# A transformer block on one core: the first transfer joined with part of x^T, and the norm of attention B one step behind its products

## The chip, the core and the metric

The kernel runs on one core of a Trainium2 chip. The metric is device time in microseconds (us) of one execution, as the median over several runs. The changed kernel is compared with the kernel before on the same chip.

## What is computed

One layer of an encoder block on a sequence of 512 rows of 1024 (S = 512, D = 1024), all in float32. Cut to what matters:

```python
proj = u @ w_in                          # [q_a|k_a|v_a | q_b|k_b|v_b | g], 5120 columns
o_a  = chunked_relbias_attention(q_a, k_a, v_a, rel_bias)     # 8 heads of 64
# attention B: 4 heads, two softmax maps each, values 128 wide
s1, s2 = q1 @ k1.T * scale, q2 @ k2.T * scale   # q, k with partial rotary, masked by chunk
w    = softmax(s1) - lam * softmax(s2)
o_b  = rms_norm(w @ v_b, subln_g) * (1.0 - lam_init)          # per head and row
gates = sigmoid(g + b_gate)
mix  = (g_a * (o_a @ w_branch_a) + g_b * (o_b @ w_branch_b)) @ w_out
x    = LN1(alpha * x + mix)
x    = LN2(alpha * x + relu(x @ w_ff1)**2 @ w_ff2)
```

## The kernel before, in words

**Products in three parts.** Every float32 operand is split into a high and a low part (`split`, lines 83 to 87: ACT casts, line 84; DVE subtracts, line 85), and a product is the sum of three matmuls: high by high, high by low, low by high (`tmm`, lines 184 to 186, with the weights held; `smm`, lines 189 to 191, with the activations held). The weights are one stream `w` of chunks of 128 x 1024 in the order of their use. `prefetch` loads and splits them ahead (tiles `raw`, `wh`, `wl`, three buffers each); `chunk` hands out the next. In a group by `smm` (`s_group`) four row tiles run over blocks of x^T of 128 rows (tiles X): block 0 for all four row tiles, then block 1, and so on, so the first 12 matmuls use block 0.

**The start.** `warm_up(7)` (line 252) sends seven matmuls of zeros. `first_loads` issues, on ACT's queue, the first 128 columns of block 0 of x^T (line 113), and on SP's queue the first half of chunk 0, the other 384 columns of that block, the second half of chunk 0, block 1, and so on. `split_x` splits block 0 in two pieces (line 100), since the first products need only 128 columns of it.

**The main line of work** is `proj` (values of A, then four pairs of query and key of A, queries, keys and values of B, eight pairs of gates, and branch A), a generator that stops after every 12 matmuls or so. `advance(n)` lets it do n such steps. The attention's steps are put between: 36 steps of `attn_a`, then `attn_b`, with PACE = 1.8 steps of the main line to each (line 678). The engines work in order. A scheduler puts each engine's instructions in order at build time, starting from the order of the code; it may move one ahead of or behind its neighbours on the same engine.

**Attention B** (`attn_b`, lines 505 to 583) has 16 units (head h, row tile t). Unit i is begun in step i: two score products (277, 278), for each map the sum with the mask and its maximum (`softexp`, line 285, DVE), Exp (287, ACT) and reciprocal (289, DVE); then the second map times lam/sum: a scalar product on DVE (563), a scaling on POOL (564), and the combination on DVE (565). LAG = 3 steps later `prob_transpose` transposes the result on PE (296) and splits it (303 ACT, 304 DVE). In the unit t = 2 of a head `prep_b` transposes the queries and keys of the next (500) and `stack` splits them (261 ACT, 262 DVE).

Two further stages follow once the last row tile of a head is through. Stage 1, one step later, is `pv` (520 to 522): the products with the values, and from them on ACT the square twice (525, and 526 as `sq_h`) and `og` (528), and on DVE the low part of the square, `sq_l` (529). Stage 3, two steps behind that, is `normalise`: two matmuls with `ones_r` (536), the first over `sq_h`, the second over `sq_l`, give the mean square in every row; then Sqrt on ACT (537, with a load of its function table before and one after, for Exp), the reciprocal on DVE (538, 3.35 us), the product with `og` (541) and its split. The loop:

```python
for stage in (3, 1):
    k = i - LAG - stage
    if 0 <= k < len(units) and k % NT == NT - 1:
        h = units[k][0]
        if stage == 1:
            held[h] = pv(h)
        else:
            normalise(*held.pop(h))
```

Of the kernel before, what the change touches and what calls it, by code (L numbers as in the profile page):

```python
# [9 lines left out]
F32 = mybir.dt.float32  # L10
# [6 lines left out]
P = 128  # L17
# [23 lines left out]
def block_kernel(ctx, tc, w, x_t, x, pos, relb, bgate, lq1, lk1, lq2, lk2, subg,  # L41
# [56 lines left out]
    def split_x(k):  # L98
        h, l, raw = xt(FR), xt(FR), x_raw.pop(k)
        for lo, hi in ((0, P), (P, S)) if k == 0 else ((0, S),):  # L100
            split(raw[:, lo:hi], h[:, lo:hi], l[:, lo:hi])
        xh.append(h)
        xl.append(l)
# [7 lines left out]
    def first_loads():  # L111

        load_x(0, ((0, P),), A)
        for i in range(2):
            raws[i] = wp.tile([P, 1024], F32, tag="raw", bufs=3, name=name("raw"))
            for j in range(2):
                sl = slice(512 * j, 512 * (j + 1))
                nc.sync.dma_start(out=raws[i][:, sl], in_=w[i][:, sl])
                load_x(2 * i + j, ((P, S),) if i + j == 0 else ((0, S),))
        dma_at[0] = 2  # L120

    def prefetch(n_dma, n_split):
# [5 lines left out]
        while split_at[0] < min(NCH, n_split):  # L128
# [7 lines left out]
            else:  # L136
                h = wp.tile([P, 1024], FR, tag="wh", bufs=3, name=name("wh"))
                l = wp.tile([P, 1024], FR, tag="wl", bufs=3, name=name("wl"))
                if i < 2:
                    for j in range(2):  # L140
                        sl = slice(512 * j, 512 * (j + 1))
                        split(raws[i][:, sl], h[:, sl], l[:, sl])
                        split_x(2 * i + j)
                else:
                    split(raws[i], h, l, G if i in on_pool else V)
# [42 lines left out]
    def smm(ps, ah, al, w_h, w_l, first, last):  # L188
        T.matmul(ps, ah, w_h, start=first, stop=False)  # L189
        T.matmul(ps, ah, w_l, start=False, stop=False)  # L190
        T.matmul(ps, al, w_h, start=False, stop=last)  # L191
# [313 lines left out]
    def attn_b():  # L505
# [44 lines left out]
        for i in range(len(units) + LAG + 4):  # L550
# [24 lines left out]
            for stage in (3, 1):  # L575
# [100 lines left out]
    for _ in range(16 + LAG + 4):  # L676
        next(steps_b, None)
        due += PACE
        advance(int(due))
        due -= int(due)  # L680
# [259 lines left out]
def _layout(x, positions, w_in, b_gate, rel_bias, lambda_q1, lambda_k1, lambda_q2, lambda_k2,  # L940
            subln_g, w_branch_a, w_branch_b, w_out, ln1_g, ln1_b, w_ff1, w_ff2, ln2_g, ln2_b):
    a = {k: np.asarray(v) for k, v in locals().items()}
    idx = np.clip(384 + np.arange(P)[:, None] - np.arange(S)[None, :], -128, 128) + 128
    return {
        "w": _weight_stream(a["w_in"][0], a["w_branch_a"][0], a["w_branch_b"][0], a["w_out"][0],
                            a["w_ff1"][0], a["w_ff2"][0]),
        "x_t": a["x"][0].T,
# [29 lines left out]
```

## Time and profile before

| what | value |
|---|---|
| median of 3 runs | 736.63 us (736.24 to 737.06) |
| the profiled execution, its own time | 734.53 us |
| its span on the core | 732.7 us |
| mean granted clock of TensorE | 0.996 of full speed |
| busy: PE / DVE / ACT / POOL | 98% / 59% / 40% / 12% |

The page of the profile gives the busy time of each engine (PE is TensorE's matmuls, PEld its weight loads, DVE VectorE, ACT ScalarE, POOL GpSimd, SP the engine that issues most transfers). The waits list says which instruction of an engine stood idle for which instruction of another. The timeline lists instructions by their start; the names in it are the program's tiles without their numbers, and L529 is line 529 of the kernel. A matmul of 512 columns shows some 0.39 us in the timeline although the next starts 0.23 us later, since neighbours overlap.

### The profile page before, as it was taken

To read this page: it belongs to the slowest core of one execution; us is meant where nothing else is said; L and a number is where in the kernel's file an instruction comes from. 1 tells how busy PE (TensorE), PEld (TensorE's weight loads), DVE (VectorE), ACT (ScalarE), POOL (GpSimd) and SP (SyncE) were. 2 spreads that over 40 slices of the span, in tenths; PEclk is the share of its full clock that TensorE was granted. 3 is DMA by queue.
4 is the path that set the end of the run, shared out by engine and by line. 5 is a ranking of instruction groups with operands and counts; after the bars stand their busy time and mean duration, and the time that the engine had idled before them with its cause. 6 is when DMAs were issued, how large, how long until landed. Compare 5 with 4: busy or idle time off the path is not lost.

```text
span 732.7 us, 9157 instructions
## 1 busy us (share of the span) xinstructions
PE 721.3 (98%) x3415; PEld 603.0 (82%) x3415; DVE 432.0 (59%) x788; ACT 295.7 (40%) x512; POOL 89.3 (12%) x119
## 2 busy tenths in 40 slices
PE   9999999999999999999999999999999999999995
PEld 7888888888887888888898888888888888888885
DVE  6676655547667767655877885423225655622545
ACT  6465654546567755334453322212112322312200
POOL 0022323231433120042000000000000000000001
PEclk9999999999999999999999999999999999999998
DMA  8663222222332313364213223233232223232302
GB/s 291 212 181 100 87 87 65 80 87 84 111 94 76 98 58 115 125 249 159 73 59 111 79 98 115 87 97 104 87 109 92 87 86 115 90 111 87 116 29 87
DMA packets 27085, 78.35 MB, mean 107 GB/s; under 512 B 4384, under 2 KB 5152, under 8 KB 27040
## 3 DMA queue, kind: packets, MB, share of 16 engines
q1 hardware_dynamic: 26176, 76.64, 32.0%
q10 hardware_dynamic: 864, 1.11, 0.4%
q8 instruction: 27, 0.44, 0.2%
q14 instruction: 18, 0.15, 0.1%
HBM read 71.45 MB, written 2.10 MB: 100 GB/s over the span
## 4 chain that ended last, share of the span: by engine, by line
PE 95%; DVE 2%; ACT 1%; issue 1%; DMA 0%; POOL 0%; DVEq 0%; POOLq 0%; ACTq 0%
PE mm L184 11%; PE mm L186 11%; PE mm L185 11%; PE mm L189 9%; PE mm L190 9%; PE mm L191 9%; PE st L190 4%; PE st L191 4%; PE st L189 4%; PE st L185 3%; PE st L184 3%; PE st L186 3%; PE o L190 2%; PE o L191 1%; PE o L189 1%; PE st L278 1%
## 5 line engine op out<-in xcount | busy, mean ns | idle before, releaser
L85 DVE TENSOR_TENSOR wl<-raw,wh 128x1024 fp32r<-128x1024 f32 (+1 forms) x116 | 140.2, 1209 | 121.7 <-ACT wh L84 121.4
L84 ACT CAST wh<-raw 128x1024 fp32r<-128x1024 f32 (+1 forms) x116 | 120.1, 1035 | 193.7 <-PE st L191 67.1
L189 PE MATMUL mm<-wh,X 128*128 128x512 f32 (+1 forms) x192 | 76.7, 400 | 1.1 <-ACT wh L84 0.8
L184 PE MATMUL mm<-X,wh 128*128 128x512 f32 x192 | 76.9, 401 | 0.0
L185 PE MATMUL mm<-X,wh 128*128 128x512 f32 x192 | 75.0, 390 | 0.0
L186 PE MATMUL mm<-X,wl 128*128 128x512 f32 x192 | 74.9, 390 | 0.0
L190 PE MATMUL mm<-wl,X 128*128 128x512 f32 (+1 forms) x192 | 74.5, 388 | 0.0
L191 PE MATMUL mm<-wh,X 128*128 128x512 f32 (+1 forms) x192 | 74.4, 388 | 0.0
L186 PE MATMUL mm<-x1t_h,wl 128*128 128x512 f32 x128 | 49.8, 389 | 0.0
L185 PE MATMUL mm<-x1t_l,wh 128*128 128x512 f32 x128 | 49.8, 389 | 0.0
L184 PE MATMUL mm<-x1t_h,wh 128*128 128x512 f32 x128 | 49.8, 389 | 0.0
L287 ACT ACTIVATE e<-e,s 128x128 f32<-128x128 f32 (+3 forms) x64 | 36.1, 564 | 33.6 <-DVE s L285 32.1
L771 POOL TENSOR_SCALAR s<-s 128x1 f32<-128x1 f32 x1 | 0.4, 409 | 388.2 <-DVE s L755 388.2
L379 POOL TENSOR_SCALAR e<-e,s 128x128 f32<-128x128 f32 (+3 forms) x32 | 34.7, 1086 | 84.5 <-DVE s L289 84.5
L189 PEld LDWEIGHTS mm<-wh,X 128*128 128x128 f32 x192 | 36.1, 188 | 8.7 <-ACT wh L84 1.3
L186 PEld LDWEIGHTS mm<-X,wl 128*128 128x128 f32 x192 | 36.1, 188 | 7.8
L191 PEld LDWEIGHTS mm<-wh,X 128*128 128x128 f32 x192 | 36.1, 188 | 7.6
L184 PEld LDWEIGHTS mm<-X,wh 128*128 128x128 f32 x192 | 36.1, 188 | 6.9
L185 PEld LDWEIGHTS mm<-X,wh 128*128 128x128 f32 x192 | 36.1, 188 | 6.6
L190 PEld LDWEIGHTS mm<-wl,X 128*128 128x128 f32 x192 | 36.2, 188 | 6.5
L84 ACT CAST V<-lt 128x512 fp32r<-128x512 f32 x24 | 14.9, 620 | 62.5 <-DVE lt L849 62.5
L186 PE MATMUL st<-x1t_h,wl 128*128 128x512 f32 (+1 forms) x104 | 38.8, 373 | 0.0
(254 smaller groups left out, 1545.8 us busy)
## 6 DMA issues: line engine op xcount, KB each, us to landing
raw<-in_w_dram SPq DMA_DIRECT2D x118, 512.0 KB, 3.3
q<-q SPq DMA_DIRECT2D x32, 128.0 KB, 2.3
G<-in_relb_dram SPq DMA_DIRECT2D x8, 256.0 KB, 4.6
x<-in_x_dram SPq DMA_DIRECT2D x4, 512.0 KB, 6.5
e<-in_x_t_dram SPq DMA_DIRECT2D x7, 256.0 KB, 6.3
raw<-in_w_dram SPq DMA_DIRECT2D x4, 256.0 KB, 4.6
out_dram<-x SPq DMA_DIRECT2D x3, 256.0 KB, 2.1
out_dram<-x ACTq DMA_DIRECT2D x3, 256.0 KB, 2.1
```

The source lines that it names most:

```text
L84: A.copy(out=h, in_=src)
L85: i = (eng or V).tensor_tensor(out=l, in0=src, in1=h.bitcast(F32), op=ALU.subtract)
L184: T.matmul(ps, lw_h, rh, start=first, stop=False)
L185: T.matmul(ps, lw_h, rl, start=False, stop=False)
L186: T.matmul(ps, lw_l, rh, start=False, stop=last)
L189: T.matmul(ps, ah, w_h, start=first, stop=False)
L190: T.matmul(ps, ah, w_l, start=False, stop=False)
L191: T.matmul(ps, al, w_h, start=False, stop=last)
L278: T.matmul(ps[:, :n], q2[:, sl], k1[:, :n], start=False, stop=True)
L287: A.activation(e[:, :n], e[:, :n], AF.Exp, bias=nm, scale=-1.0, accum_out=sums)
L379: G.tensor_scalar(ex[:, :n], ex[:, :n], r, None, op0=ALU.mult)
L771: G.tensor_scalar(nmr, mv[:, 0:1], -1.0, None, op0=ALU.mult)
```

## The change

Three edits.

1. **The first transfer.** A new input `w_x` holds, side by side, the first half of chunk 0 (512 columns) and the first 128 columns of block 0 of x^T. One transfer of 640 columns on SP's queue brings both into the tile `raw` of chunk 0; the transfer on ACT's queue is gone. The second half of chunk 0 goes into a tile of its own (`half`). `first_split` casts the 128 columns of x and half of the weights on DVE, the other half of the weights on ACT; the subtractions follow on DVE.
2. **The order in `smm`**: high by high, low by high, high by low.
3. **The norm of attention B** moves from stage 3 to stage 2, one step behind `pv`, and the loop is one step shorter.

The diff, cut to its core:

```diff
     def split_x(k):
         h, l, raw = xt(FR), xt(FR), x_raw.pop(k)
-        for lo, hi in ((0, P), (P, S)) if k == 0 else ((0, S),):
-            split(raw[:, lo:hi], h[:, lo:hi], l[:, lo:hi])
+        split(raw, h, l)
...
     def first_loads():
-        load_x(0, ((0, P),), A)
         for i in range(2):
             raws[i] = wp.tile([P, 1024], F32, tag="raw", bufs=3, name=name("raw"))
             for j in range(2):
                 sl = slice(512 * j, 512 * (j + 1))
-                nc.sync.dma_start(out=raws[i][:, sl], in_=w[i][:, sl])
-                load_x(2 * i + j, ((P, S),) if i + j == 0 else ((0, S),))
+                if i + j == 0:
+                    nc.sync.dma_start(out=raws[0][:, 0:640], in_=w_x)
+                    half.append(e_tile())
+                    load_x(0, ((P, S),))
+                elif i == 0:
+                    nc.sync.dma_start(out=half[0], in_=w[0][:, sl])
+                    load_x(1)
+                else:
+                    nc.sync.dma_start(out=raws[i][:, sl], in_=w[i][:, sl])
+                    load_x(2 * i + j)
...
+    def first_split(h, l):
+        raw, x0h, x0l = raws[0], xt(FR), xt(FR)
+        V.tensor_copy(out=x0h[:, 0:P], in_=raw[:, 512:640])
+        A.copy(out=h[:, 0:256], in_=raw[:, 0:256])
+        V.tensor_copy(out=h[:, 256:512], in_=raw[:, 256:512])
+        V.tensor_tensor(out=x0l[:, 0:P], in0=raw[:, 512:640], in1=x0h[:, 0:P].bitcast(F32),
+                        op=ALU.subtract)
+        V.tensor_tensor(out=l[:, 0:512], in0=raw[:, 0:512], in1=h[:, 0:512].bitcast(F32),
+                        op=ALU.subtract)
+        split(x_raw.pop(0)[:, P:S], x0h[:, P:S], x0l[:, P:S])
...
+        split(half.pop(), h[:, 512:1024], l[:, 512:1024])
+        split_x(1)
...
     def smm(ps, ah, al, w_h, w_l, first, last):
         T.matmul(ps, ah, w_h, start=first, stop=False)
-        T.matmul(ps, ah, w_l, start=False, stop=False)
-        T.matmul(ps, al, w_h, start=False, stop=last)
+        T.matmul(ps, al, w_h, start=False, stop=False)
+        T.matmul(ps, ah, w_l, start=False, stop=last)
...
-        for i in range(len(units) + LAG + 4):
+        for i in range(len(units) + LAG + 3):
...
-            for stage in (3, 1):
+            for stage in (2, 1):
...
-    for _ in range(16 + LAG + 4):
+    for _ in range(16 + LAG + 3):
...
+        "w_x": np.concatenate([w[0][:, 0:512], x_t[0:P, 0:P]], 1),
```

The lines of the changed kernel stand 27 further down from `smm` on (line 529 before is 556 after, 536 is 563, 565 is 592). What the scheduler makes of edit 3 shows in the orders of the engines.

PE in head 0 of attention B before, behind the scores of a unit of head 1 (st) and the transposes of the same step (L296); the rows behind them are gate products:

```order
L277 MATMUL st_2431<-q_2282,q_2271 128x128
L278 MATMUL st_2431<-q_2282,q_2288 128x128
L296 MATMUL mm_2445<-ident,e_2198 128x128 x2
L184 MATMUL mm_2450<-X_136,wh_2172 128x512
L185 MATMUL mm_2450<-X_137,wh_2172 128x512
L186 MATMUL mm_2450<-X_136,wl_2173 128x512
```

The same place with the change:

```order
L304 MATMUL st_2432<-q_2283,q_2272 128x128
L305 MATMUL st_2432<-q_2283,q_2289 128x128
L323 MATMUL mm_2446<-ident,e_2199 128x128 x2
L563 MATMUL mm_2451<-V_2370,ones_r 128x512
L563 MATMUL mm_2451<-V_2371,ones_r 128x512
L211 MATMUL mm_2462<-X_134,wh_2173 128x512
L212 MATMUL mm_2462<-X_135,wh_2173 128x512
L213 MATMUL mm_2462<-X_134,wl_2174 128x512
```

The two ones-products (L563; V are the two parts of the square) now stand straight behind the transposes, ahead of the gate products, which follow unmoved.

Where the pair stood before on PE, one step further down, behind three transposes:

```order
L277 MATMUL st_2493<-q_2282,q_2271 128x256
L278 MATMUL st_2493<-q_2282,q_2288 128x256
L296 MATMUL mm_2507<-ident,e_2242 128x128 x3
L536 MATMUL mm_2513<-V_2369,ones_r 128x512
L536 MATMUL mm_2513<-V_2370,ones_r 128x512
L184 MATMUL mm_2536<-X_136,wh_2384 128x512
L185 MATMUL mm_2536<-X_137,wh_2384 128x512
```

With the change these transposes (L323) are followed by the gate products at once; 24 gate products lie between the two places.

DVE in head 2 before, around the last unit's softmax (L285, L289), the scalar of its second map (L563), the low part of the square (L529) and the combination (L565, which reads what POOL scaled in line 564):

```order
L289 RECIPROCAL s_2927<-s_2924 128x1
L285 ISA e_2932,s_2933<-st_2929,maskb 128x512
L285 ISA s_2933 128x1
L289 RECIPROCAL s_2937<-s_2934 128x1
L563 TENSOR_SCALAR s_2939<-s_2937,lam 128x1
L529 TENSOR_TENSOR V_2964<-e_2962,V_2963 128x512
L565 SCALAR_TENSOR_TENSOR e_2922<-e_2922,s_2927,e_2932 128x512
L85 TENSOR_TENSOR wl_2998<-raw_2989,wh_2997 128x1024
```

The same place with the change (L316 is 289 before, L312 is 285, L331 is 304, L590 is 563, L592 is 565, L556 is 529):

```order
L316 RECIPROCAL s_2928<-s_2925 128x1
L312 ISA e_2933,s_2934<-st_2930,maskb 128x512
L312 ISA s_2934 128x1
L331 TENSOR_TENSOR pl_2945<-mm_2946,ph_2944 128x128
L316 RECIPROCAL s_2938<-s_2935 128x1
L590 TENSOR_SCALAR s_2940<-s_2938,lam 128x1
L592 SCALAR_TENSOR_TENSOR e_2923<-e_2923,s_2928,e_2933 128x512
L556 TENSOR_TENSOR V_2965<-e_2963,V_2964 128x512
L85 TENSOR_TENSOR wl_3010<-raw_3001,wh_3009 128x1024
```

The low part of the square has moved from ahead of the combination to behind it. In head 0 it stands behind the combination in both kernels, in head 1 the change puts it ahead of the reciprocal and the scalar.

DVE at the start before (X_136 and X_137 are the high and low parts of block 0 of x^T, X_145 the low part of block 1):

```order
L249 MEMSET e_101 128x128
L85 TENSOR_TENSOR X_137<-e_110,X_136 128x128
L85 TENSOR_TENSOR wl_133<-raw_112,wh_132 128x512
L85 TENSOR_TENSOR X_137<-e_110,X_136 128x384
L85 TENSOR_TENSOR wl_133<-raw_112,wh_132 128x512
L85 TENSOR_TENSOR X_145<-e_116,X_144 128x512
```

And with the change (X_134 and X_135 are block 0 now, X_146 the low part of block 1):

```order
L276 MEMSET e_101 128x128
L134 CAST X_134<-raw_110 128x128
L136 CAST wh_132<-raw_110 128x256
L137 TENSOR_TENSOR X_135<-raw_110,X_134 128x128
L139 TENSOR_TENSOR wl_133<-raw_110,wh_132 128x512
L85 TENSOR_TENSOR X_135<-e_113,X_134 128x384
L85 TENSOR_TENSOR wl_133<-e_112,wh_132 128x512
L85 TENSOR_TENSOR X_146<-e_116,X_145 128x512
```

Two casts and one subtraction now stand ahead of the first low part of the weights (wl); the low part of block 1 is still last.

## Rows read from the trace of the kernel before

**Rows 1.** The page, part 1: busy us of each engine, share, instructions.
```profile
PE 721.3 (98%) x3415; PEld 603.0 (82%) x3415; DVE 432.0 (59%) x788; ACT 295.7 (40%) x512; POOL 89.3 (12%) x119
```
**Rows 2.** Waits of PE: waiter <- releaser: us in all, times, longest.
```profile
PE mm L296 <- DVE pl L304: 1.4, 1, 1.4
PE st L252 <- DVE e L249: 1.0, 1, 1.0
PE mm L189 <- ACT wh L84: 0.8, 1, 0.8
```
**Rows 3.** DMA issues of the first 3 us: KB each, median us to landing.
```profile
raw<-in_w_dram SPq DMA_DIRECT2D x1, 256.0 KB, 3.2
e<-in_x_t_dram ACTq DMA_DIRECT2D x1, 64.0 KB, 3.4
...
e<-in_x_t_dram SPq DMA_DIRECT2D x1, 256.0 KB, 4.5
```
**Rows 4.** Timeline of the start: start us, us, engine, instruction, idle time before it.
```profile
4.11 0.30 ACT L84 CAST X<-e 128x128 fp32r<-128x128 f32 x1 [1.67 <-DMA e<-in_x_t_dram]
4.32 0.61 ACT L84 CAST wh<-raw 128x512 fp32r<-128x512 f32 x1
...
4.98 0.92 PE L189 MATMUL mm<-wh,X 128*128 128x512 f32 x2 [0.77 <-ACT wh L84]
...
7.33 0.69 DVE L85 TENSOR_TENSOR X<-e,X 128x512 fp32r<-128x512 f32 x1
...
8.32 0.39 PE L190 MATMUL mm<-wl,X 128*128 128x512 f32 x1
```
**Rows 5.** Groups of DVE by form: busy us, mean ns, idle before.
```profile
L440 DVE COPY cos_t<-cos_t 128x32 f32<-128x32 f32 x1 | 0.2, 180 | 0.6 <-ACT cos_t L436 0.6
L442 DVE COPY cos_t<-cos_t 128x64 f32<-128x64 f32 x1 | 0.2, 196 | 0.0
```
**Rows 6.** Timeline: head 0's reciprocal, and PE's wait behind it.
```profile
227.99 3.35 DVE L538 RECIPROCAL e<-e 128x512 f32<-128x512 f32 x1 [1.08 <-ACT e L537]
...
236.76 0.33 PE L296 MATMUL mm<-ident,e 128*128 128x128 f32 x1 [1.37 <-DVE pl L304]
```
**Rows 7.** Timeline: POOL and DVE in head 0, up to `sq_l`.
```profile
216.37 1.56 POOL L564 TENSOR_SCALAR e<-e,s 128x512 f32<-128x512 f32 x1 [7.44 <-DVE s L563]
217.97 0.94 DVE L565 SCALAR_TENSOR_TENSOR e<-e,s,e 128x512 f32<-128x512 f32 x1 [1.79 <-POOL e L564]
218.83 0.80 DVE L529 TENSOR_TENSOR V<-e,V 128x512 fp32r<-128x512 f32 x1
```
**Rows 8.** Timeline of PE in head 0: the new place of the pair, and the old.
```profile
217.24 0.48 PE L184 MATMUL mm<-X,wh 128*128 128x512 f32 x1
...
223.52 0.72 PE L536 MATMUL mm<-V,ones_r 128*128 128x512 f32 x2
224.08 0.40 PE L184 MATMUL mm<-X,wh 128*128 128x512 f32 x1
```
**Rows 9.** Timeline of PE, DVE and POOL in head 2.
```profile
269.62 0.48 PE L184 MATMUL mm<-X,wh 128*128 128x512 f32 x1
...
271.24 0.69 DVE L529 TENSOR_TENSOR V<-e,V 128x512 fp32r<-128x512 f32 x1
271.36 2.00 POOL L564 TENSOR_SCALAR e<-e,s 128x512 f32<-128x512 f32 x1 [4.82 <-ACT V L526]
...
273.39 0.75 DVE L565 SCALAR_TENSOR_TENSOR e<-e,s,e 128x512 f32<-128x512 f32 x1 [1.47 <-POOL e L564]
```
**Rows 10.** Timeline: first scores of head 2's last unit, and their softmax.
```profile
264.03 0.39 PE L278 MATMUL st<-q,q 128*128 128x512 f32 x1
...
267.12 0.68 DVE L285 CUSTOM_DVE_ANT_0 e<-st,maskb 128x512 f32<-128x512 f32 x1
```
**Rows 11.** Busy us by stretch (PE, PEld, DVE, ACT, POOL), PE's granted clock, DMA share, GB/s.
```profile
237.00:239.00 2.00, 2.00 (x14) 1.86 (x14) 1.91 (x5) 1.98 (x5) 0.25 (x1) 1.00 0.91 199
```
**Rows 12.** Timeline of PE: the warm-up.
```profile
1.04 3.17 PE L252 MATMUL st<-e 128*128 128x512 f32 x7 [1.04 <-DVE e L249]
```

More of the change, by code (lines that the diff above doesn't have):

```diff
@@ L40, in block_kernel @@
 @with_exitstack
-def block_kernel(ctx, tc, w, x_t, x, pos, relb, bgate, lq1, lk1, lq2, lk2, subg,
+def block_kernel(ctx, tc, w, w_x, x_t, x, pos, relb, bgate, lq1, lk1, lq2, lk2, subg,
                  ln1_g, ln1_b, ln1_gt, ln1_bt, ln2_g, ln2_b, out):
@@ L117, in first_loads @@
                 sl = slice(512 * j, 512 * (j + 1))
-                nc.sync.dma_start(out=raws[i][:, sl], in_=w[i][:, sl])
-                load_x(2 * i + j, ((P, S),) if i + j == 0 else ((0, S),))
-        dma_at[0] = 2
+                if i + j == 0:
[8 more added lines that the diff above has]
+                    load_x(2 * i + j)
+        dma_at[0] = 2
+    half = []
+    def first_split(h, l):
[8 more added lines that the diff above has]
+        split(x_raw.pop(0)[:, P:S], x0h[:, P:S], x0l[:, P:S])
+        xh.append(x0h)
+        xl.append(x0l)
+        split(half.pop(), h[:, 512:1024], l[:, 512:1024])
+        split_x(1)
     def prefetch(n_dma, n_split):
@@ L138, in prefetch @@
                 l = wp.tile([P, 1024], FR, tag="wl", bufs=3, name=name("wl"))
-                if i < 2:
+                if i == 0:
+                    first_split(h, l)
+                elif i == 1:
                     for j in range(2):
@@ L943, in _layout @@
     idx = np.clip(384 + np.arange(P)[:, None] - np.arange(S)[None, :], -128, 128) + 128
+    w = _weight_stream(a["w_in"][0], a["w_branch_a"][0], a["w_branch_b"][0], a["w_out"][0],
+                       a["w_ff1"][0], a["w_ff2"][0])
+    x_t = a["x"][0].T
     return {
-        "w": _weight_stream(a["w_in"][0], a["w_branch_a"][0], a["w_branch_b"][0], a["w_out"][0],
-                            a["w_ff1"][0], a["w_ff2"][0]),
-        "x_t": a["x"][0].T,
+        "w": w,
+        "w_x": np.concatenate([w[0][:, 0:512], x_t[0:P, 0:P]], 1),
+        "x_t": x_t,
         "x": a["x"][0],
```

## The prediction

> **What bounds the kernel now.** I read the page's busy times first, then the waits of PE, then the timelines of PE, DVE, ACT and POOL at the few places where PE waits. PE is busy for 721.3 of 732.7 us [rows 1]: nearly everything is TensorE work, and only what makes PE start later or stand still can move the end. PE has three waits of over half a us [rows 2]: 1.0 us before the warm-up matmuls, 0.8 us before the first real one, and 1.4 us once in attention B. (The rest of its idle time is the tail behind the last matmul, which the change leaves alone.) So at most 0.8 us at the start and 1.4 us in attention B are to be had, and the question is which new waits come.
>
> The profiled execution took 734.53 us, 732.7 of it span; the median of the runs shown is 736.63, 2.10 above. I make the sum against 734.53 and add the 2.10 at the end. About 0.2% (1.5 us) is what a measurement of this kernel tells from no change.
>
> **Part 1, the start.** Before, 128 columns of `x^T` are issued on ACT's queue and land 3.4 us later, and the first half chunk on SP's lands 3.2 us after its issue [rows 3]. ACT casts x at 4.11 (0.30 us), then the half chunk at 4.32 (0.61 us), and PE's first product starts at 4.98, 0.05 behind the cast's end [rows 4]. The change puts both in one transfer of the same bytes. I let it land at 4.1, as x does. ACT then casts 256 columns, which takes between 0.30 (for 128) and 0.61 (for 512), say 0.4, while DVE casts 128 and then 256. A one-source DVE copy takes 180 ns for 32 columns and 196 for 64 [rows 5], 0.5 ns a column: 0.23 and 0.29 us by that. PE's first product could start at 4.1 + 0.23 + 0.29 + 0.05 = about 4.7, 0.3 us earlier.
>
> It does not keep all of that. In the new order the second product of each three takes the low part of x, so the second product of the second block of x (the 14th in all) needs that low part; before, only the 15th did. The block comes by an unchanged transfer, 4.5 us on its way [rows 3], and its low part is made at 7.33 and ready at 8.02 [rows 4]. PE can therefore run its 14th at 8.07, against 8.32 before [rows 4]. **Term 1: -0.25 us**, bounds 0 (the one transfer lands as late as 4.5 us) and -0.4. Elsewhere the new order has two products of three swapped, the same matmuls and weight loads: nothing.
>
> **Part 2, the norm of attention B.** It moves the two ones-products (line 536) of heads 0 to 2 forward by one unit, ahead of 24 matmuls of the gate projection, and with them Sqrt and its two table loads on ACT and the 3.35 us reciprocal on DVE. No instruction is added but one table load behind the last head, on an ACT with idle time there. The saving: in head 0 the reciprocal at 227.99 stands on DVE in front of the subtraction (line 304) for which PE waits until 236.76 [rows 6]. With the reciprocal some 5 us earlier (24 matmuls at the mean of 721.3 / 3415 = 0.21 [rows 1]) that subtraction is not late any more. **Term 2: -1.37 us**, bounds 0 and -1.37.
>
> The price: the second ones-product reads `sq_l`, which DVE makes in line 529. DVE and PE both work in order, and what stands in front of line 529 decides. In head 0 the order up to there is unchanged: POOL's product (line 564, 1.56 us), DVE's combination (line 565), then line 529 at 218.83, ready at 219.63 [rows 7]. Before, PE needs it behind 223.52, almost 4 us later [rows 8]: hidden. Now PE comes to the pair straight behind its transposes, where the gate product of 217.24 stood [rows 8]. A pair takes 0.56 (223.52 to 224.08 [rows 8]), so the second is due at 217.52 and waits until 219.68. Everything behind it on PE waits too: gate products, scores, transposes. **Term 3: +2.1 us**, bounds +1.5 and +2.7 (PE and DVE some tenths apart).
>
> Head 1: line 529 now stands ahead of the wait for POOL, and PE has 24 gate matmuls (5 us) between the head's products and the pair. I expect no wait there.
>
> Head 2 is worse. Only 12 matmuls lie between its products and the new place, so that PE arrives at 269.62 [rows 9]; and in the new order of DVE line 529 has slipped behind line 565, which waits for POOL. Before, line 529 ran at 271.24, while POOL took 2.00 us from 271.36, and line 565 ended at 273.39 + 0.75 = 274.14 [rows 9]. POOL's same product takes 1.56 us in head 0, when DVE stands idle [rows 7]; with the change nothing of DVE runs beside it here either, so I take 1.56 (2.00 is the other bound). A rule of the Trainium skill goes the same way: GpSimd shares its SBUF interfaces with VectorE and contends with DVE instructions of two SBUF inputs (GPSIMD Engine Reference, section 1, Specifications). So: POOL ends at 272.92, line 565 at 273.70, line 529 at 274.39, and the second ones-product starts at 274.44. The gate product that stood at 269.62 follows 0.23 later, at 274.67; without any wait it would stand at 269.62 + 0.56 = 270.18. **PE is then 4.5 us late in all**, terms 2 and 3 included. This takes DVE's clock as it was, because from head 0 to here it has the same instructions to do and runs behind PE: it begins head 2's last softmax at 267.12, where the scores were there from 264.03 + 0.39 = 264.42 [rows 10].
>
> Bounds. Upper: 2.00 us for POOL, +4.9. Lower: DVE has caught up with PE before head 2 and starts at 264.45, 2.7 us sooner. Then, with PE late by 2.1 - 1.4 = 0.7 from head 0, it is 4.5 - 2.7 + 0.7 = +2.5. I take 4.5, from the rows as they stand.
>
> Head 3 has 24 matmuls of the branch in between and no POOL: no wait. After that PE has no waits in which its lateness could vanish [rows 2].
>
> **Sum.** 734.53 - 0.25 + 4.5 = 738.8 for a profiled execution; as a median 736.63 - 0.25 + 4.5 = **740.9 us**.
>
> **The rivals.**
> 1. Faster: no ones-product waits, and the 1.37 and the 0.25 are gained: 735.0. For it: line 529 is short itself (0.8 us [rows 7]) and would be in time if DVE took it while POOL works. Against it: in heads 0 and 2 it stands behind line 565 and so behind POOL. It decides if line 529 ends 2.1 us earlier than in the row. Chance 0.08.
> 2. Only head 0 waits: 736.63 + 2.1 - 1.37 - 0.25 = 737.1. This needs DVE to be over 4 us earlier at head 2 than before. The reciprocals of heads 0 and 1 lie 5 us earlier there, which is for it; the work in front of head 2 stays the same, and the scores come no sooner than PE makes them, which is against. Chance 0.14.
> 3. The clock falls. PE stands still for longer than ever in this trace: some 2 us in head 0 and up to 3.8 in head 2. After the one wait of 1.37 us the granted clock is 1.00 [rows 11], so up to there a wait costs only itself. The warm-up at the start took 3.17 us for 7 products [rows 12], 0.45 each, the rate of 1.2 GHz, against 0.21 [rows 1]; a relapse as long as that costs 7 x 0.24 = 1.7 us: 742.6. Chance 0.12. A rule of the Trainium skill says that it happens (TensorE: Matmul & The Clock Gate, HAM oscillation): a PE kept waiting between bursts of matmuls falls to half its clock and starts the next burst cold. This trace has no wait in its middle that shows it.
> 4. The start does not do what it says: one transfer of 320 KB lands late. That costs 0.25 us and is in the range of every case.
>
> **How the numbers follow.** The forecast (heads 0 and 2 wait) has 0.66, with its own range 738.7 (736.63 - 0.4 + 2.5) to 741.5 (736.63 + 4.9); rivals 1 to 3 as above. The range from 736.8 to 742.6 takes in the forecast, rival 2 and most of rival 3, and leaves out rival 1. Faster by over 0.2%: rival 1, 0.08. Within 0.2%: rival 2, 0.14. Slower: forecast and rival 3, 0.78.
>
> **What would show it.** Right: PE's waits name DVE's line 529 before the ones-products, about 2 us in head 0 and 2 to 4 in head 2; the wait of 1.4 before the transposes is gone; the first real product starts near 4.7 and the 14th near 8.07. Wrong: ones-products without a wait, or line 529 ahead of POOL's product in heads 0 and 2. A granted clock below 1.00 behind head 2's wait would be rival 3.

## The result, and the profile after

The changed kernel takes **742.76 us** (median of 5 runs, 741.12 to 743.12), the kernel before 736.44 us (5 runs, 735.03 to 737.06) on the same chip: a ratio of 1.0088, with a 95% interval of 1.0072 to 1.0103. It is slower by 6.3 us. Forecast were 740.9 us in a range of 736.8 to 742.6: the direction was right, the time lies 0.16 us outside.

The profiled execution of the change took 742.76 us, the median itself, with a span of 741.0 us. Against the profiled execution before (span 732.7) that is 8.3 us, 2 more than between the medians; the runs below show where these 2 us come from (the start).

The page of the changed kernel, part 1, which answers to [rows 1]:

```profile
PE 724.3 (98%) x3415; PEld 604.0 (82%) x3415; DVE 432.0 (58%) x790; ACT 296.7 (40%) x512; POOL 87.3 (12%) x119
```

The matmuls are the same in number; PE is busy 3.0 us longer and ACT 1.0, POOL 2.0 us shorter, DVE the same. The waits of PE (waiter <- releaser: us in all, times, longest), which answer to [rows 2]:

```profile
PE mm L563 <- DVE V L556: 4.4, 2, 2.3
PE mm L563 <- ACT V L553: 1.2, 1, 1.2
PE st L279 <- DVE e L276: 1.0, 1, 1.0
PE mm L213 <- DVE wl L85: 0.8, 1, 0.8
PE mm L216 <- ACT X L84: 0.6, 1, 0.6
...
PE mm L323 <- DVE pl L331: 0.2, 1, 0.2
```

The ones-products (L563) now wait for the low part of the square (L556) in two places, 4.4 us in all, and once for its high part (L553, on ACT); there is a new wait for `wl`; the 1.4 us before the transposes (L323) have shrunk to 0.2. At the start the wait before the first product is gone, and one of 0.6 us before the third has come (L216, for the rest of the first block of x^T).

**Where the time went.** I laid the two timelines of PE side by side and took, at the same instruction, the start after less the start before; between the new and the old place of a pair, its 0.56 us [rows 8] are taken off.

| place on PE (start before) | start after | late by, us |
|---|---|---|
| 14th product (8.32) | 8.79 | +0.47, then +0.37 up to head 0 |
| gate product behind head 0's new pair (217.24) | 220.75 | +2.95 |
| the same behind its old place (224.08) | 226.93 | +2.85 |
| last transposes of head 0 (236.76) | 238.51 | +1.75 |
| gate product that needs `wl` (258.79) | 261.50 | +2.71 |
| gate product behind head 2's new pair (269.62) | 276.82 | +6.64 |
| gate product behind its old place (275.99) | 284.19 | +8.20 |
| end of the span (732.7) | 741.0 | +8.3 |

Five steps make it: the start, a stall in head 0, 1.1 us back, a wait for `wl`, a stall in head 2, and then 1.5 us more without any wait. Behind head 2 PE is late for good. The rows, first the stall in head 0 on POOL's and DVE's side and on PE's (timeline of the changed kernel: start, us, engine, instruction, idle time before it):

```profile
216.69 0.21 DVE L590 TENSOR_SCALAR s<-s,lam 128x1 f32<-128x1 f32 x1
...
218.70 0.93 DVE L592 SCALAR_TENSOR_TENSOR e<-e,s,e 128x512 f32<-128x512 f32 x1 [1.79 <-POOL e L591]
...
219.55 0.80 DVE L556 TENSOR_TENSOR V<-e,V 128x512 fp32r<-128x512 f32 x1
...
220.41 0.50 PE L563 MATMUL mm<-V,ones_r 128*128 128x512 f32 x1 [2.35 <-DVE V L556]
```

This is term 3 as it was drawn: DVE waits 1.79 us for POOL, then combines, then makes `sq_l`, and PE waits 2.35. The same timeline further on, with the 1.1 us back and the wait for `wl`:

```profile
237.76 0.69 DVE L331 TENSOR_TENSOR pl<-mm,ph 128x512 fp32r<-128x512 f32 x1
...
238.51 0.33 PE L323 MATMUL mm<-ident,e 128*128 128x128 f32 x1 [0.17 <-DVE pl L331]
...
261.50 0.50 PE L213 MATMUL mm<-X,wl 128*128 128x512 f32 x1 [0.81 <-DVE wl L85]
```

Head 2, which answers to [rows 9]:

```profile
273.10 0.21 DVE L590 TENSOR_SCALAR s<-s,lam 128x1 f32<-128x1 f32 x1
...
273.48 1.56 POOL L591 TENSOR_SCALAR e<-e,s 128x512 f32<-128x512 f32 x1 [4.59 <-DVE s L590]
...
273.89 0.50 PE L563 MATMUL mm<-V,ones_r 128*128 128x512 f32 x1 [1.20 <-ACT V L553]
...
275.08 0.75 DVE L592 SCALAR_TENSOR_TENSOR e<-e,s,e 128x512 f32<-128x512 f32 x1 [1.76 <-POOL e L591]
...
275.75 0.68 DVE L556 TENSOR_TENSOR V<-e,V 128x512 fp32r<-128x512 f32 x1
...
276.49 0.50 PE L563 MATMUL mm<-V,ones_r 128*128 128x512 f32 x1 [2.09 <-DVE V L556]
```

PE stands still for 1.20 us, does one product, and stands still for 2.09 more. And then its clock is down (stretches of the changed kernel, columns as in [rows 11], the granted clock third from the end):

```profile
277.00:279.00 2.00, 2.00 (x7) 1.52 (x7) 1.67 (x3) 1.97 (x3) 0.00 (x0) 0.57 0.14 31
279.00:281.00 2.00, 2.00 (x7) 1.56 (x6) 2.00 (x1) 0.50 (x1) 0.00 (x0) 0.57 0.63 231
```

Granted clock 0.57, and 7 products in 2 us (10 in the run below that fills the wait): the lower level of 1.2 GHz for most of the time up to 280.7. In the timeline eight steps from product to product, from 277.29 to 280.68, take 3.39 us instead of 1.8 (eight times 0.23), which is the last 1.5 us. A rule of the Trainium skill (TensorE: Matmul & The Clock Gate, HAM oscillation) says that a PE that waits too long between bursts of matmuls falls to half its clock. This trace agrees, though in three places (below) a single wait of 2.0 to 2.35 us left the clock at 1.00.

### The profile page after: what moved, and what is told of

Same layout as the page of the kernel before. It is cut to its first block, busy times and chain, and to the rows that moved or that the text cites. A ratio compares the mean times of both kernels' runs of the same rounds, so it can differ in the third digit from the quotient of the medians.

```text
span 741.0 us, 9163 instructions
## 1 busy us (share of the span) xinstructions
PE 724.3 (98%) x3415; PEld 604.0 (82%) x3415; DVE 432.0 (58%) x790; ACT 296.7 (40%) x512; POOL 87.3 (12%) x119
## 4 chain that ended last, share of the span: by engine, by line
PE 88%; DVE 5%; ACT 2%; issue 2%; POOL 2%; DMA 1%; SPq 0%; DVEq 0%; POOLq 0%; ACTq 0%
PE mm L211 9%; PE mm L213 9%; PE mm L212 9%; PE mm L216 8%; PE mm L217 8%; PE mm L218 8%; PE st L216 4%; PE st L218 4%; PE st L217 4%; PE st L211 3%; PE st L213 3%; PE st L212 3%; POOL e L591 2%; PE o L216 1%; PE o L218 1%
## 5 line engine op out<-in xcount | busy, mean ns | idle before, releaser
L85 DVE TENSOR_TENSOR wl<-raw,wh 128x1024 fp32r<-128x1024 f32 (+1 forms) x114 | 138.4, 1214 | 120.5 <-ACT wh L84 120.4
L216 PE MATMUL mm<-wh,X 128*128 128x512 f32 (+1 forms) x192 | 76.8, 400 | 0.9 <-ACT X L84 0.6
L216 PEld LDWEIGHTS mm<-wh,X 128*128 128x128 f32 x192 | 36.1, 188 | 9.0 <-ACT X L84 1.5
```

The costliest lines, as they stand in the source:

```text
L85: i = (eng or V).tensor_tensor(out=l, in0=src, in1=h.bitcast(F32), op=ALU.subtract)
```

## The experiments

Lateness is read as in the table above. "Time" is the median less that of the kernel before in the same session (736.2 to 736.6).

### The parts alone

e1 is the change with this taken back (and both loops at LAG + 4 again); e2 is the kernel before with this alone made (and both loops at LAG + 3):

```diff
-            for stage in (3, 1):
+            for stage in (2, 1):
```

> The change without its third edit (norm of attention B back at stage 3): first transfer and order of the three products alone. Theory (the joined transfer lands early, but the second block of x^T now lands later, so the 14th product waits for its low part): first product near 4.2, 14th near 8.8 against 8.32 before, from there some 0.4 us late to the end; time +0.4 us against the kernel before, and PE waits 1.4 us again in head 0. Rival (the late second block was an accident of one execution): 14th near 8.07, time -0.25 us.

> The kernel before with the third edit alone. Theory (the stalls of heads 0 and 2, a wait for wl between them, and the clock's fall behind head 2 all come from the moved norm): from the aligned traces +2.6 - 1.1 + 1.1 + 3.8 + 1.5 = about +7.9 us in the profile, waits of some 2.3 us in head 0 and over 3 in head 2, granted clock below 1.00 behind head 2. Rival (the late start pushed VectorE and makes part of it): at most +4.8, as forecast for this part, and no wait for wl.

**Start alone: 735.62 us (11 runs), ratio 0.9990 (0.9981 to 0.9999), -1.0 us.** Neither expectation: the profile shows the first product at 4.34 and the 14th at 9.13, later than before as the theory has it, and yet the median is lower. **Norm alone: 742.90 us (4 runs), ratio 1.0094 (1.0079 to 1.0108), +6.3 us**; its profile has the waits of the whole change (2.0 in head 0, 0.83 for `wl`, 1.23 and 2.09 in head 2) and a granted clock of 0.50 from 278 to 280 (waits in all, then the stretch):

```profile
PE mm L536 <- DVE V L529: 4.1, 2, 2.1
PE mm L536 <- ACT V L526: 1.2, 1, 1.2
...
278.00:280.00 2.00, 2.00 (x6) 1.52 (x6) 1.67 (x2) 1.72 (x2) 0.00 (x0) 0.50 0.57 217
```

So the loss is the norm's: it is all there without the changed start. If the start's gain added to it, the whole change would lie 1.0 us below e2; both have +6.3, and their intervals leave open which of the two it is. What the start does is a question by itself.

### What is `sq_l` waiting for?

e3 is e2 with the combination (line 565) emitted behind the stages and, in the last unit of a head, held in program order:

```diff
-                V.scalar_tensor_tensor(out=e1[:, :n], in0=e1[:, :n], scalar=r1, in1=e2[:, :n],
-                                       op0=ALU.mult, op1=ALU.subtract)
...
+            if i < len(units):
+                c = V.scalar_tensor_tensor(out=e1[:, :n], in0=e1[:, :n], scalar=r1,
+                                           in1=e2[:, :n], op0=ALU.mult, op1=ALU.subtract)
+                if t == NT - 1 and h:
+                    tc.keep_in_program_order(c)
```

> The kernel before with the third edit, and the combination of the unit in the same step moved behind sq_l, so that sq_l no longer stands behind POOL. Theory (sq_l behind POOL is what makes PE wait): no wait in head 0, in head 2 at most about 2 us (sq_l could end at 271.9 where PE comes at 270), no fall of the clock: time 0 to +2 us against the kernel before. Rival (VectorE's or ScalarE's lateness as a whole makes the wait, POOL's place does not matter): waits of 2 us and more in both heads, +5 us or more.

**736.78 us (10 runs), ratio 1.0006 (0.9996 to 1.0016).** The 6.3 us of the norm are gone. Its waits of PE:

```profile
PE mm L536 <- ACT V L526: 0.9, 1, 0.9
...
PE mm L536 <- DVE V L529: 0.4, 1, 0.4
```

In head 0 none is left; head 2 waits 0.9 us for ACT's square and 0.4 for `sq_l`. So it is the place behind POOL that made the stalls. What stays in head 2 is ACT, which works off the Exps of the last scores before it comes to the squares, and only 12 matmuls of PE cover that.

### The heads one by one

e5, e6 and e7 are the kernel before with one head moved (HEAD is 0, 2 and 1):

```diff
-            for stage in (3, 1):
+            for stage in (3, 2, 1):
...
-                    else:
+                    elif stage == (2 if h == HEAD else 3):
                         normalise(*held.pop(h))
```

> The kernel before with the norm one step earlier in head 0 alone. Theory (the wait for sq_l in head 0 is a cost of its own, and the reciprocal moved away gives 1.1 us back): a wait of 2.2 us before the second ones-product, the wait before the transposes down to 0.2, no new wait later: +2.6 - 1.1 = +1.5 us against the kernel before. Rival (the earlier norm of head 0 also pushes VectorE, which makes PE wait again at head 2 or for wl): +3 us or more, with a wait named there.

> The kernel before with the norm one step earlier in head 2 alone. Here the scheduler leaves sq_l of head 2 ahead of the combination that waits for POOL (with all heads moved it stands behind). Theory (the place behind POOL makes the large wait): sq_l ready near 271.9 on VectorE's clock of the kernel before, PE there at 269.9, a wait of about 2 us in all, no fall of the clock or a short one: +1.8 to +2.5 us. Rival (12 matmuls of cover are too few whatever the order): waits of over 3 us, clock at half behind them, +5 us.

> The kernel before with the norm one step earlier in head 1 alone. Theory (moved, head 1's reciprocal stands in front of the subtraction that makes wl, and PE waits for that; the ones-products themselves do not wait): a wait of 0.8 to 1.3 us for wl and nothing else new: about +1 us. Rival (wl was late only because PE's earlier stalls had shifted the engines against each other): no wait for wl, +-0.3 us.

**Head 0: 738.11 us, ratio 1.0027 (1.0018 to 1.0036), +1.7**, with a wait of 2.0 us for `sq_l`, as the theory has it; but one new wait does come later, 0.4 us at 278 for a subtraction of DVE (`pl`); another, of 0.8 us, lies at 41, in attention A, which this edit does not touch. **Head 2: 739.06, ratio 1.0036 (1.0024 to 1.0048), +2.7**: a little over the 1.8 to 2.5 of the theory, with no fall of the clock (1.00 from 270 to 280), and with one correction; the wait is ACT's:

```profile
PE mm L536 <- ACT V L526: 1.4, 1, 1.4
...
PE mm L536 <- DVE V L529: 0.2, 1, 0.2
```

**Head 1: 736.66, ratio 1.0002 (0.9993 to 1.0011)**, no wait for `wl`: the rival. `wl` was late in the change not because of head 1's own move; that DVE's lateness made it is likely, and not tested by itself. And in the orders of DVE `sq_l` of head 2 stands behind the combination only where head 1 is moved (e7, e2 and the change), not where head 2 alone is (e6). The heads alone come to 1.7 + 2.7 + 0.3 = 4.7 us, 1.6 less than the whole. Two things are left that only the whole has: with that order head 2 waits 3.3 us instead of 1.6, and the clock falls, for 1.5. Together they are more than 1.6, so the parts do not simply add, and which of them lose by it is not shown.

### Does the wait cost the clock?

e4 is the change with this ahead of head 2's pair:

```diff
+            for _ in range(14 if len(ob_h) == 2 else 0):
+                T.matmul(rb, ones_r, sq_h, start=True, stop=True)
```

> The changed kernel with 14 more products of ones_r and sq_h ahead of head 2's pair, 3.2 us of work into a bank that the pair then overwrites, so that PE works while it would wait for sq_l. Theory (the wait of over 3 us makes the clock fall, which costs 1.5 us): granted clock 1.00 behind head 2, time 1.5 us below that of the changed kernel, so +4.8 against the kernel before where that was +6.3. Rival (the clock falls for another reason, or its fall costs nothing): clock still 0.57 there, or the same +6.3.

**742.24 us (4 runs), ratio 1.0081 (1.0068 to 1.0095)**: 0.5 us below the change, which the intervals do not separate. The profile does. The stretch behind head 2 (columns as in [rows 11]):

```profile
278.00:280.00 2.00, 2.00 (x10) 1.68 (x9) 1.29 (x3) 1.60 (x3) 0.00 (x0) 1.00 0.45 133
```

Clock 1.00, 10 products in 2 us where the change has 7 at 0.57. Between the pair and 280.68 PE gains 1.6 us on the change; 0.9 of it had been spent, since the fourteen products, which can start only when `sq_h` is there, last longer than the wait for `sq_l` that is left then. So the fall behind head 2 is the wait's, and costs 1.5 us there; the time alone does not show it. In this execution the clock also fell behind head 0's 2.3 us:

```profile
221.50:223.00 1.50, 1.50 (x6) 1.22 (x5) 0.76 (x4) 1.48 (x4) 0.04 (x1) 0.65 0.00 0
223.00:224.50 1.50, 1.50 (x5) 1.11 (x5) 0.59 (x1) 1.47 (x3) 0.00 (x0) 0.50 0.00 0
```

It did not after 2.35 us in the change, nor after some 2.0 in e2 and e5. This fall costs 1.6 us on the spot, but PE comes to head 2 only 0.6 later than in the change (273.29 for 272.69): the wait for `wl` is not there in e4.

### What the start gains

e8 is e1 with the first of these edits, e9 the kernel before with the second:

```diff
-                    load_x(1)
+                    load_x(1, q=A)
...
-    warm_up(7)
+    warm_up(9)
```

> The changed start (norm at stage 3, as in the run with the start alone), with the second block of x^T issued on ScalarE's queue instead of fourth on SyncE's. Theory (the start is held by that block, which lands late since it is issued late): its cast some 1 us sooner, the 14th product near 8.0 instead of 8.8 to 9.1, time 0.5 to 1 us below the start alone, that is -1.5 to -2 us against the kernel before. Rival (the transfers share the same bandwidth, so it is not the issue that is late): the 14th within 0.3 of the start alone, or the first product later by as much, no gain.

> The kernel before with nine warm-up products in place of seven. Theory (between the end of the seven and the first product, at 4.95, PE stands idle for some 0.6 us, and in most executions the first products then run 0.43 us apart until 9.4; the joined transfer gains because it closes that gap): the gap is gone, the first products come 0.23 apart from 6 at the latest in every execution, median -1 to -1.5 us and the times of single executions closer together. Rival (the joined transfer gains because data come sooner): first product later by up to 0.2, time the same or +0.2 us.

**e8: 736.41 us, ratio 0.9999 (0.9990 to 1.0008)**: the rival. The first product starts at 5.43, 1.1 us later than in e1. Issued beside it, the second block costs the joined transfer its lead (DMA issues of the first us: KB each, us to landing):

```profile
raw<-in_w_x_dram SPq DMA_DIRECT2D x1, 320.0 KB, 4.1
e<-in_x_t_dram ACTq DMA_DIRECT2D x1, 256.0 KB, 4.3
```

4.1 us instead of 3.0 in e1 and 2.8 in the change. **e9: 735.48 us (11 runs), ratio 0.9987 (0.9978 to 0.9996), -0.75 us**, single runs within 0.9 us of each other (734.94 to 735.86) where those of the kernel before spread over 2.3: the theory, with no transfer changed, though less than the 1 to 1.5 us it expected. Its timeline has no gap behind the warm-up, and products 0.23 us apart soon after:

```profile
1.04 4.21 PE L252 MATMUL st<-e 128*128 128x512 f32 x9 [1.04 <-DVE e L249]
5.22 0.80 PE L189 MATMUL mm<-wh,X 128*128 128x512 f32 x1
...
6.52 0.40 PE L189 MATMUL mm<-wh,X 128*128 128x512 f32 x1
6.75 0.39 PE L190 MATMUL mm<-wl,X 128*128 128x512 f32 x1
```

e3, which has the old start, shows the other kind of execution, with products still 0.43 us apart at 9:

```profile
5.01 1.22 PE L189 MATMUL mm<-wh,X 128*128 128x512 f32 x2 [0.61 <-ACT wh L84]
...
8.59 0.63 PE L191 MATMUL mm<-wh,X 128*128 128x512 f32 x1
9.01 0.63 PE L189 MATMUL mm<-wh,X 128*128 128x512 f32 x1
```

The start of the 15th product in all profiles of this study makes it plain (the granted clock reads 1.00 in all these stretches; it is the pace that shows the 1.2 GHz):

| start | gap before the first product | 15th product starts at |
|---|---|---|
| old, seven products (8 profiles) | 0.5 to 0.8 us | 8.55, 8.88, 9.03, 9.11, 10.44, 10.52, 10.69, 10.70 |
| joined transfer (7) | none | 8.55, 8.86, 9.12, 9.27, 9.39, 9.46, 9.59 |
| old, nine products (4) | none | 8.85, 9.18, 9.51, 9.64 |
| joined transfer, second block on ACT's queue (e8) | 1.0 us | 10.98 |

With the gap behind seven products, five of nine executions run the first block at half the pace nearly to its end; without it none of eleven does (e4, e12 and e15 run about half of it so). What it is about the gap is not shown: in the change itself PE waits nearly as long two products later, and keeps the full pace behind it:

```profile
5.46 0.50 PE L216 MATMUL mm<-wh,X 128*128 128x512 f32 x1 [0.57 <-ACT X L84]
```

The profiled execution before was one of the quick four, the quickest of them (8.55): that is why it lies 2 us below its median, and why the sum against it did not show this term.

### What the moved reciprocal gives back

e10 (the changed start) and e11 (the old start, nine warm-up products) have head 0 alone at stage 2, as in e5, and its combination behind the stages; e12 is e10 with the old order of products in `smm`:

```diff
+                if (h, t) != (1, NT - 1):
...
+            if i == 2 * NT - 1:
+                tc.keep_in_program_order(
+                    V.scalar_tensor_tensor(out=e1, in0=e1, scalar=r1, in1=e2,
+                                           op0=ALU.mult, op1=ALU.subtract))
```

> The changed start, with the norm one step earlier in head 0 alone and there with sq_l ahead of the combination that waits for POOL. Theory (what head 0 costs is its place behind POOL alone, and its gain of 1.1 us stands by itself): no wait for sq_l of over 0.3 us, the 1.4 to 1.8 us before the transposes down to 0.2, no new wait: -1.0 (start) - 1.1 = -2 us against the kernel before. Rival (the wait of 1.4 turns up later, as a late subtraction at head 2): -1 us as with the start alone.

> Both: nine warm-up products and the old start, head 0 as in the run before. Theory (the clock at the start is what the joined transfer gains): as that run, -2 us against the kernel before, or a little better. Rival (sooner data): -1.1 us, 1 us behind that run.

> As the run with the changed start and head 0, with the old order of the three products (high by high, high by low, low by high). Theory (the low part of the second block of x^T is the last to be ready, and the new order asks for it one product sooner): in the profile one product fewer behind that low part, 0.2 us sooner at the same landing; in time the same within what can be measured. Rival (the new order is what lets the start run early, since the low part of the weights comes later than that of x): the third to fifth products wait, 0.2 to 0.4 us later.

**736.54, 736.56 and 735.75 us; ratios 1.0004 (0.9995 to 1.0013), 1.0003 (0.9995 to 1.0012), 0.9994 (0.9985 to 1.0003).** A gain of 2 us was expected of e10, and not even the start's 1.0 was left: my theory of the saving fell, and the rival's -1 was missed too. The wait for `sq_l` is gone as expected (0.3 is left), but the one before the transposes is not, and one of 0.4 us has come behind head 2, as the rival has it:

```profile
PE mm L323 <- DVE pl L331: 1.3, 1, 1.3
...
PE mm L211 <- DVE pl L331: 0.4, 1, 0.4
PE mm L563 <- DVE V L556: 0.3, 1, 0.3
```

e11 has the same 1.4 and 0.4, so both starts are worth the same here. Laid beside e9, which differs from it in head 0 alone, e11's PE loses 0.2 us in head 0 and 0.5 at that new wait; the medians differ by 1.1. In e12 the old order leaves out the wait for the low part of the second block. That block is cast at the same time as in e10 (7.86 for 7.85), and the 15th product starts 0.3 sooner, near the 0.2 expected; why the median is lower by 0.8 is not shown.

Two runs without the reciprocal of head 0 (and so without the division of that head's output) told whether it makes that wait:

e13 is the kernel before with this edit, e14 with head 0 moved as in e10 besides:

```diff
-            V.reciprocal(a, a)
+            if len(ob_h):
+                V.reciprocal(a, a)
```

> The kernel before without head 0's reciprocal (the computation leaves it out: the output of head 0 is divided by nothing). Theory (the 3.35 us of the reciprocal stand in VectorE's queue in front of the subtraction that PE waits for, so taking them away, unlike moving them, takes the wait away): no wait before the transposes, -1.2 to -1.4 us against the kernel before. Rival (the wait comes from the copies of queries and keys or from ScalarE, not from the reciprocal): a wait of 1 us or more stays, -0.3 us at most.

> The kernel before with head 0's norm one step earlier, sq_l ahead of the combination, and no reciprocal in head 0 (left out of the computation). Theory (moved, the reciprocal still stands ahead of that subtraction on VectorE, and this is why the wait of 1.3 us stayed in the run with head 0 alone): the wait is gone now, -1.2 us against the kernel before. Rival (the moved Sqrt and its two table loads delay the Exps and so VectorE, whatever the reciprocal does): a wait of 0.5 us or more before the transposes stays.

**e13: 734.66 us, ratio 0.9977 (0.9968 to 0.9986), -1.5; e14: 735.06, ratio 0.9988 (0.9979 to 0.9998), -1.1**, and in neither a wait before the transposes of [rows 6]. So the reciprocal makes it at its old place and at its new one. Moved earlier it still stands ahead of the same subtraction in DVE's queue, and takes the same 3.35 us. What DVE waited for from head 0's scalar to that subtraction (us in all, times, longest), in the kernel before from 216 to 236:

```profile
DVE e L565 <- POOL e L564: 3.3, 3, 1.8
DVE e L538 <- ACT e L537: 1.1, 1, 1.1
DVE s L289 <- ACT e L287: 0.9, 2, 0.6
```

And in the change from 216.7 to 237.8:

```profile
DVE e L592 <- POOL e L591: 3.3, 3, 1.8
DVE e L565 <- ACT e L564: 1.5, 1, 1.5
DVE s L316 <- ACT e L314: 1.5, 2, 0.8
```

5.3 us before, 6.3 after: DVE gains nothing and loses 1.0. It waits 0.4 longer for Sqrt, and 0.84 for an Exp late in the stretch where it did not wait before (rows of the change):

```profile
235.59 0.62 ACT L314 ACTIVATE e<-e,s 128x384 f32<-128x384 f32 x1 [2.20 <-DVE s L312]
...
236.33 0.16 DVE L316 RECIPROCAL s<-s 128x1 f32<-128x1 f32 x1 [0.84 <-ACT e L314]
```

In the kernel before DVE does other work at this place: it combines (L565, 233.64), makes the low part of the normalised output (L85, 234.05) and one subtraction for the next head (L262, 234.76), and the Exp is through by then. With the norm moved, the first two are done before that softmax begins and the third comes later, and the wait is uncovered.

Three more runs looked for the way in which the norm would have to move:

e16 has nine warm-up products and head 0's norm at stage 4 (both loops at LAG + 5), e17 the same norm with the changed start and order of products. e18 has nine warm-up products, the norm at stage 3, and this:

```diff
-            V.reciprocal(a, a)
+            for c in range(0, S, P):
+                V.reciprocal(a[:, c:c + P], a[:, c:c + P])
```

> Nine warm-up products, and head 0's norm one step LATER than before (stage 4) instead of earlier, which puts its reciprocal behind the subtraction for head 0's last transposes. Theory (the reciprocal costs where it stands in front of a subtraction that PE waits for; nothing needs its result soon, so later is the right way): the wait of 1.4 us before the transposes gone, up to 0.5 us of it found again behind the reciprocal's new place; -0.75 - 1 = about -1.8 us against the kernel before. Rival (a reciprocal of 3.35 us in front of any of VectorE's work in this stretch makes PE wait as long): a new wait of 1 us or more, -0.7 us as with the nine products alone.

> The changed start and order of products, with head 0's norm one step later (stage 4) and heads 1 and 2 as before the change. Theory: as the run with nine warm-up products and the later norm, -1.8 us against the kernel before. Rival: a new wait behind the reciprocal's new place, -0.7 to -1 us as with the start alone.

> Nine warm-up products, and the reciprocal cut into four of 128 columns, norm at its old step. Theory (its place on VectorE is what counts, and the pieces still stand together ahead of the subtraction): as the nine products alone, -0.75 us, the wait of 1.4 us stays or grows by the pieces' overhead. Rival (the single long instruction is what holds the engine): the wait falls to under 0.7 us, -1.4 us.

**e16: 737.06, ratio 1.0013 (1.0005 to 1.0022); e17: 736.60, ratio 1.0008 (0.9999 to 1.0017)**: the rival in kind, but worse than its -0.7 to -1: +0.8 and +0.4. The old wait is gone, others stand in its place, 2.5 us in e16:

```profile
PE mm L184 <- DVE pl L304: 1.6, 2, 1.2
...
PE st L277 <- DVE s L285: 0.9, 1, 0.9
```

**e18: 735.75, ratio 0.9994 (0.9986 to 1.0003)**: cut in four, the wait stays (1.5 us). It is the engine's time that is short here, not the length of one instruction.

### Do start and norm add?

e15 is the whole change with e3's edit:

```diff
-                V.scalar_tensor_tensor(out=e1[:, :n], in0=e1[:, :n], scalar=r1, in1=e2[:, :n],
-                                       op0=ALU.mult, op1=ALU.subtract)
...
+            if i < len(units):
...
```

> The whole change with the combinations of the units behind sq_l, as in the run with sq_l first, but with the changed start. Theory (the two parts add where PE is not held by VectorE): 736.8 of that run less the 1.0 of the start, 0.5 to 1 us below the kernel before. Rival (VectorE's and ScalarE's clock at head 2 sets PE's lateness, so that what PE gains at the start is given back there in a longer wait for the squares): as that run, 0 to +0.4 us, with a longer wait at head 2 than its 1.3 us.

**735.96 us (11 runs), ratio 1.0003 (0.9994 to 1.0012)**: not shown either way. e3, in another session, has 1.0006 (0.9996 to 1.0016), so the two are not told apart, and the 0.5 to 1 us below the kernel before that the theory wants are not there. The waits at head 2 are the same 0.9 and 0.4, against the rival; but before head 0's last transposes PE now waits 0.6 us where it waited 0.2 in e3, which takes back part of what an early PE gains.

Of the kernels that compute the whole block (e13 and e14 do not), e9 (nine warm-up products) and e1 (the start alone) are the only ones below the one before by more than their interval, by 0.13 and 0.10%.

## Why the prediction was wrong, step by step

- **The main mechanism was right.** The second ones-product waits for `sq_l` behind POOL in heads 0 and 2 and not in head 1; e3 takes it away by that order alone. Term 3 was 2.1 and came to 2.35 of wait (2.6 of lateness). POOL's 1.56 us in head 2 came as taken.
- **The step that failed: "This takes DVE's clock as it was."** In head 2 DVE's scalar (line 563) ran at 270.95 before and 273.10 after, 2.15 us later, and the second ones-product at 276.49 instead of 274.44. Of these 2.15 us 0.73 were there ahead of head 0 (215.96 to 216.69), 1.0 came with the moved norm up to head 0's last subtraction (236.02 to 237.76), the rest from there to head 2. The rows of the kernel before:

```profile
215.96 0.21 DVE L563 TENSOR_SCALAR s<-s,lam 128x1 f32<-128x1 f32 x1
...
236.02 0.69 DVE L304 TENSOR_TENSOR pl<-mm,ph 128x512 fp32r<-128x512 f32 x1
...
270.95 0.21 DVE L563 TENSOR_SCALAR s<-s,lam 128x1 f32<-128x1 f32 x1
```

  The argument was that DVE has the same instructions to do. It has, but its idle time is not the same: in their new order they no longer fill its waits for Sqrt and for an Exp (6.3 us of waits for 5.3). PE was 6.6 us late behind head 2 instead of 4.25 (4.5 less the start's 0.25).
- **Rival 3 came on top**, with 1.5 us for the forecast 1.7. I gave it 0.12 beside the forecast, though its condition, a longer wait than any in the trace, was part of the forecast itself; it belonged into the sum, or at least into the upper end of the range. Against the medians the account then closes, if the start's gain adds: 740.9, and 1.4 for DVE (2.15 without the 0.73 that came with the late start of this profile), and 1.5 for the clock, less 0.75 for a start that gains 1.0 instead of 0.25, is 743.05 for a measured 742.76. The first two alone carry the time past the end of the range.
- **Term 2 was near in size and wrong in kind.** The 1.37 us before the transposes shrank to 0.17, and PE got 1.1 us back. But the subtraction came no sooner (236.02 before, 237.76 after): PE was late by then, and a late PE waits less. Where PE is in time (e10) the wait stays. It was lateness absorbed; the forecast took it for a saving. Since it read head 2 from DVE's rows, neither this term nor term 3 entered its 4.5, and the error cost the sum nothing; in rivals 1 and 2 it did enter.
- **Two waits were left out.** The one for `wl` (0.81): e7 shows that head 1's move alone does not make it; that it is DVE's lateness once more is argued, not shown. And the one for ACT's square at head 2 (1.20): POOL's row at 271.36 in [rows 9] names it (ACT V L526) as the last to come, long after PE's 269.62. It ends before `sq_l` is there, so it cost the sum nothing, but it is what stays in e3 and e6 when `sq_l` comes early.
- **Term 1 had the wrong cause.** In the profile the first product came sooner than forecast (4.20 for 4.7) and the 14th later (8.79 for 8.07), because the second block of x^T, an unchanged transfer, landed 0.8 us later (5.3 us on its way instead of 4.5). In the median the start gains 1.0 us. That this is the closed gap behind the warm-up fits e9, which closes it with no transfer changed and gains 0.75, and e8, which has a gap again and gains nothing. The one profile that the sum was made against was a quick execution and could not show it; its distance of 2.10 us from the median was the hint, and I only added it back.

## What to carry to other kernels

A moved step takes its engine time along: moving it earlier frees nothing for what stands behind both places on the same engine, and it can uncover waits that other work had filled. A wait of the bound engine that vanishes while that engine runs late is no gain. And where the profiled execution lies away from the median, ask first which part of it was quick.

## What was not expected of the hardware

- With a gap of 0.5 to 0.8 us between seven warm-up products and the first product the executions fall in two groups, 1.3 us or more apart at the 15th product; with two more warm-up products of zeros the slower group was not seen (4 profiles, and 11 times within 0.9 us).
- A wait of 2.0 to 2.35 us left the clock at 1.00 in three profiles (e2, e5 and the change), and behind 2.35 us in a fourth (e4) it fell to 0.50; a wait of 1.2 and one of 2.1 us with a single product between them took it to 0.57 and 0.50 in both profiles that have them (the change and e2).
- A transfer of 320 KB at the start took 2.8 to 3.0 us in seven profiles, and 4.1 in the one with another of 256 KB issued beside it on a second queue.
